# A decoder block on one core: the first stage reads weights, transposes x and starts the projection in another order

## The chip, the core and the metric

The kernel runs on one NeuronCore of a Trainium2 chip. The core has five engines, each with an instruction stream of its own: TensorE (PE, matrix products; the loads of its stationary operand are shown apart as PEld), VectorE (DVE), ScalarE (ACT), GpSimd (POOL) and SyncE (SP), which here only issues DMA transfers. An engine takes its instructions in the order in which they were written for it; they wait for each other through semaphores. The metric is the device time of one execution in microseconds (us).

## The reference

One layer of a hybrid decoder block, for 1024 tokens of width 1024, in float32:

```python
mod = (silu(c) @ w_ada + b_ada)                     # six rows of 1024: sh_a, sc_a, gt_a, sh_m, sc_m, gt_m
h = rms_norm(x, g_attn_pre) * (1 + sc_a) + sh_a
proj = h @ w_in                                     # 1024 -> 2304: qa ka va qb kb vb
... rotary, sliding-window attention A (with sinks), dilated mixture B ...
mixed = concat([rms_norm(oa, g_mix_a), rms_norm(ob, g_mix_b)]); y = mixed @ w_out
x = x + gt_a * rms_norm(y, g_attn_post)
h = rms_norm(x, g_mlp_pre) * (1 + sc_m) + sh_m
y = square(relu(h @ w_up)) @ w_down
x = x + gt_m * rms_norm(y, g_mlp_post)
```

The change touches only what stands first: `sh_a` and `sc_a` (two rows of the product with `w_ada`), the modulated and normalised `h`, and the first sixth of `h @ w_in`.

## The kernel before

The order of all instructions is made by a list scheduler in the kernel's own text (`Sched`): every step is given an engine (or a choice of two), an estimated duration, the steps that it waits for and the buffers that it takes and gives back (`Res`); the scheduler plays the plan through on those estimates and writes the instructions out in the order that results. On the chip each engine then keeps that order whatever the real durations are. TensorE's steps lie in named streams ("xt", "mod", "misc", "dense", "post", "s", "pv" and others), of which the scheduler takes one at a time.

Products in full float32 precision are made of split operands: each operand is written as a high part (`F32R`, a rounded copy) and a low part (the difference), and a product takes three TensorE products, high x high, high x low and low x high (`proj_mm`, lines 769 to 774). For one block of 128 tokens and one chunk k of 128 input channels these are three products of 384 columns, from lines 771, 772 and 774. A projection unit u has 8 blocks and 8 chunks, so 192 of them; there are six units, each with 384 of the 2304 columns.

The first stage (lines 414 to 671) works in these steps:

- `load_x`, `load_ada`, `load_w`: SP brings in the eight blocks of x (512 KB each), the two needed column groups of `w_ada` for each of 8 chunks (1 MB each, two transfers), and the first unit's weights (192 KB each). `load_ada(k)` has four buffers, x has five.
- `x_block(tb)`: ACT squares and sums a block (line 553), DVE and POOL make the reciprocal root (lines 409 and 412), DVE scales the block (558), TensorE transposes it in eight pieces (568, tile `pxt`). For the first five blocks (`FIRST = 5`) ACT copies the pieces to `xnT` (573).
- `mod_chunk(k)`: scale and shift of 128 channels are sums over 1024 rows of `w_ada`. For chunk 0 TensorE does all of them (16 products of one column in the text, line 615, tile `pm`). For chunks 1 to 7 TensorE does two of eight row groups (4 products), DVE multiplies and adds the other six into `acc_a` (lines 626 and 628, 42 instructions of 256 elements), and TensorE sums `acc_a` over partitions with two products against ones (635). DVE finishes scale and shift (640, 641). ACT then modulates five blocks of the chunk (645), ACT writes the high part (651), POOL the low part (654), and the first unit's weights are split by ACT (473) and POOL (478).
- `first_unit`: five accumulators, one bank of PSUM each, take chunk after chunk as its parts come ready (tile `acc`).
- Blocks 5 to 7 of x follow when all chunks are known: they are modulated at the transpose (580, 583) and split whole (593, 596); their 72 projection products are the first tiles of `proj_tile` (tile `pj`).

`evac` empties each finished block (rotary, splitting, transposes to `pq` and `pk` at lines 724 and 736), after which attention for it can begin (scores `s_ps` at line 997, weights `p_sb`, transposes `pt_ps`, outputs `o_ps`). `todo_dense` feeds the remaining projection tiles between the attention work. `next_unit_w` loads and splits the next unit's weights.

Of the kernel before, what the change touches and what calls it, by code (L numbers as in the profile page):

```python
# [10 lines left out]
F32 = mybir.dt.float32  # L11
# [292 lines left out]
def hybrid_block(ctx: ExitStack, tc: tile.TileContext, x, positions, w_ada, b_ada, g_attn_post, w_in, w_out,  # L304
# [110 lines left out]
    FIRST = 5  # L415
# [4 lines left out]
    xnT = p0.tile([P, KC, FIRST * P], F32, name="xnT")  # L420
    r_wa, r_xs, r_acc = Res(4), Res(2), Res(3)
# [6 lines left out]
    e_c = load(lambda: nc.sync.dma_start(head[:], consts[:, 0:HEAD]), 106496, prio=pri())  # L428
    wa_t, wa_e, sent = {}, {}, {}

    def load_ada(k):
        def emit():
            wa_t[k] = p0.tile([P, KC, 2, P], F32, name="wa", tag="wa", bufs=4)
            for i in range(2):
                nc.sync.dma_start(wa_t[k][:, :, i], ada_view[:, :, i * D + k * P:i * D + (k + 1) * P])

        def issued():
            sent[k].t = 0.0
        sent[k] = Ev()
        wa_e[k] = load(emit, 1048576, takes=[(r_wa, 1)], prio=pri(), after=issued)  # L440
# [3 lines left out]
    def load_x(tb, deps=()):  # L444
        r = r_stg if tb % 2 == 0 else r_xs

        def emit():
            x_t[tb] = stage("x_sb") if tb % 2 == 0 else p0.tile([P, D], F32, name="x_sb", tag="x_sb", bufs=2)
            nc.sync.dma_start(x_t[tb][:], x[tb * P:(tb + 1) * P])
        x_e[tb] = load(emit, 524288, deps, takes=[(r, 1)], prio=pri())  # L450
# [3 lines left out]
    def load_w(u, k, prio=None, deps=()):  # L454
# [13 lines left out]
        w_rawe[u, k] = load(emit, 196608, deps, takes=[(r_wst, 1)], prio=pri() if prio is None else prio)  # L468

    def split_w(u, k):  # L470
# [10 lines left out]
        if u == 0:  # L481
            w_e[u, k] = op("POOL", t_ptt(UW), lo(G), [e], gives=[(r_wst, 1)], prio=3)
        else:
            w_e[u, k] = op(("DVE", "POOL"), (t_dv(UW), t_ptt(UW)), (lo(V), lo(G)), [e], gives=[(r_wst, 1)], prio=3)

    for tb in range(2):
        load_x(tb)
    e_posi = load(lambda: nc.sync.dma_start(posi[:], positions), 4096, prio=pri())
    load_ada(0)
    for tb in range(2, FIRST):  # L490
        load_x(tb)
    load_w(0, 0)
    for k in range(1, KC):
        load_ada(k)
        load_w(0, k)
    for tb in range(FIRST, TB):
        load_x(tb, [sent[KC - 2 if tb == FIRST else KC - 1]])

    e_init = op("DVE", 0.3, lambda: (V.memset(ones[:], 1.0), V.memset(nhalf[:], -0.5)), prio=0)
# [40 lines left out]
    def f_sin():  # L540
# [3 lines left out]
    e = op("ACT", 3.0, f_sin, [e], prio=8)  # L544
    e_rope = op("DVE", 0.15, lambda: V.tensor_scalar(sinw[:, :, 0], sinw[:, :, 1], -1.0, None, ALU.mult), [e],
                prio=8)

    e_xn = []

    def x_block(tb):  # L550
# [8 lines left out]
        box, eh, d_all, evs_ = {}, [], [], []  # L559

        def hv():
            return x_t[tb][:].rearrange("p (k t) -> p k t", k=KC)
        r_x_ = r_stg if tb % 2 == 0 else r_xs
        for g in range(2):
            def tr(g=g):
                box[g] = pt.tile([P, 4, P], F32, name="pxt", tag="t")
                for k in range(4):
                    T.transpose(box[g][:, k], x_t[tb][:, (4 * g + k) * P:(4 * g + k + 1) * P], ident)
            d = pe_op("xt", 0.7, tr, [e], takes=[(r_t, 1)], gives=[(r_x_, 1)] if g and tb < FIRST else [])
            d_all.append(d)  # L570
            if tb < FIRST:
                def ev(fn, g=g):
                    return lambda: fn(xnT[:, 4 * g:4 * g + 4, tb * P:(tb + 1) * P], box[g][:])
                e_xn.append(op("ACT", t_ps(512), ev(A.copy), [d], gives=[(r_t, 1)], prio=2))
            else:
                def ev(eng, g=g):
                    def f():
                        for k in range(4 * g, 4 * g + 4):
                            if eng is A:
                                A.activation(hv()[:, k], box[g][:, k - 4 * g], AF.Identity,  # L580
                                             bias=s_a[:, k:k + 1], scale=g_a[:, k:k + 1])
                            else:
                                V.tensor_scalar(hv()[:, k], box[g][:, k - 4 * g], g_a[:, k:k + 1],
                                                s_a[:, k:k + 1], ALU.mult, ALU.add)
                    return f
                evs_.append((d, ev))
        for d, ev in evs_:

            eh.append(op(("ACT", "DVE"), (1.4, 1.3), (ev(A), ev(V)), d_all + [e_gs[k] for k in range(KC)],
                         gives=[(r_t, 1)], prio=1))  # L590
        if tb >= FIRST:
            def hi(fn):
                return lambda: fn(hw[:, tb, 0], x_t[tb][:])

            def lo(eng):
                return lambda: eng.tensor_tensor(hw[:, tb, 1], x_t[tb][:], hw[:, tb, 0].bitcast(F32), ALU.subtract)
            e = op(("ACT", "DVE"), (t_sb(D), t_d2(D)), (hi(A.copy), hi(V.tensor_copy)), eh, prio=1)
            e2 = op(("DVE", "POOL"), (t_dv(D), t_ptt(D)), (lo(V), lo(G)), [e], gives=[(r_x_, 1)], prio=1)
            e_h[tb] = [e, e2]

    e_gs, e_h, e_hh, e_hl = {}, {}, {}, {}
    NF0 = FIRST * P
    ADA_PE = (8, 2, 2, 2, 2, 2, 2, 2)

    def mod_chunk(k):
        b = {}
        e = None
        jp = ADA_PE[k]
        ej = None

        def pm0():
            b["ps"] = px.tile([P, 2], F32, name="pm", tag="x")
            for i in range(2):
                for j in range(jp):
                    T.matmul(b["ps"][:, i:i + 1], wa_t[k][:, j, i], cond[:, j:j + 1], start=(j == 0), stop=(j == jp - 1))  # L615
        if jp:
            e = pe_op("mod", 0.426 * jp, pm0, [wa_e[k], e_cond], takes=[(r_x, 1)],
                      gives=[(r_wa, 1)] if jp == KC else [])
            if jp < KC:
                ej = op("DVE", 0.07, lambda: V.tensor_tensor(bb[:, k], bb[:, k], b["ps"][:], ALU.add), [e, e_cols],  # L620
                        gives=[(r_x, 1)], prio=1)
        for j in range(jp, KC):
            def f(j=j):
                if j == jp:
                    b["acc"] = p0.tile([P, 2, P], F32, name="acc_a", tag="acc_a", bufs=3)
                    V.tensor_scalar(b["acc"][:], wa_t[k][:, j], cond[:, j:j + 1], None, ALU.mult)
                else:
                    V.scalar_tensor_tensor(b["acc"][:], wa_t[k][:, j], cond[:, j:j + 1], b["acc"][:], ALU.mult, ALU.add)  # L628
            e = op("DVE", 0.4 if j > jp else 0.26, f, [wa_e[k], e_cond] if j == jp else [e] + ([ej] if ej and j == KC - 1 else []),
# [1320 lines left out]
```

## Time and profile before

| | us |
|---|---|
| median of three runs | 1196.32 |
| lowest, highest | 1194.2, 1199.15 |
| the profiled execution | 1197.14 |
| its span, first to last instruction | 1195.4 |
| PE busy, PEld busy | 1143.5, 998.0 |
| DVE, ACT, POOL busy | 881.3, 666.6, 264.6 |

In the rows of the profile a group of instructions is named by its line in the kernel, engine, operation, the tile it writes and those it reads, the shape and how often it occurs. In the order of time, the first number is the start in us from the span's start and the second the length of the merged row; what stands in brackets is the idle time of the engine just before and what ended it. In the views by stretches each engine's busy time in the stretch is given with the number of its instructions; PEclk is the share of full speed that TensorE's clock was granted.

### The profile page before, as it was taken

How to read it: one execution, taken by the hardware profiler on the slowest of the kernel's cores; microseconds unless marked ns; L12 is line 12 of the kernel's file. 1: busy time of each engine (PE TensorE's matmuls, PEld its weight loads, DVE VectorE, ACT ScalarE, POOL GpSimd, SP SyncE). 2: the span in 40 equal slices, each digit the busy share in tenths (PEclk: the TensorE clock that was granted, in tenths of full speed). 3: DMA queues.
4: the chain of work that ended last, by engine and by line, in shares of the span. 5: the costliest groups of instructions: out<-in, count | busy, mean ns of one | idle time of the engine just before them, and what ended most of it. 6: DMA issues, size and time to landing. Idle time of an engine off the chain costs nothing.

```text
span 1195.4 us, 17424 instructions
## 1 busy us (share of the span) xinstructions
PE 1143.5 (96%) x6064; PEld 998.0 (83%) x6064; DVE 881.3 (74%) x1794; ACT 666.6 (56%) x1411; POOL 264.6 (22%) x325
## 2 busy tenths in 40 slices
PE   7879999999998998999899999999999999999996
PEld 6869999989998896888688888888888888888885
DVE  4977667666789897667888955479763797646998
ACT  6457666556666787667657533473325643246542
POOL 6534655465655333111100000000000000000002
PEclk9889999999999999999999999999999999999999
DMA  9621333213231422555296126952268511586103
GB/s 290 189 60 60 89 98 97 77 52 102 76 87 54 125 53 77 179 201 204 113 381 246 36 73 238 340 168 62 81 218 284 191 36 53 179 287 220 36 19 141
DMA packets 104423, 166.53 MB, mean 139 GB/s; under 512 B 11152, under 2 KB 56336, under 8 KB 104336
## 3 DMA queue, kind: packets, MB, share of 16 engines
q1 hardware_dynamic: 104336, 165.42, 41.8%
q8 instruction: 48, 0.79, 0.3%
q14 instruction: 39, 0.32, 0.1%
HBM read 137.08 MB, written 28.31 MB: 138 GB/s over the span
## 4 chain that ended last, share of the span: by engine, by line
PE 76%; DVE 13%; issue 4%; ACT 3%; POOL 3%; DMA 1%; SPq 0%; DVEq 0%; POOLq 0%; ACTq 0%
PE mlp_ps L1773 16%; PE mlp_ps L1774 16%; PE mlp_ps L1772 16%; PE pj L771 4%; PE pj L774 3%; PE pj L772 3%; PE s_ps L997 3%; PE o_ps L1131 1%; PE pt_ps L1100 1%; DVE acc_a L628 1%; PE y_ps L1348 1%; PE y_ps L1350 1%; PE pm L615 1%; PE y_ps L1349 1%; PE pt_ps L1103 1%
## 5 line engine op out<-in xcount | busy, mean ns | idle before, releaser
L1772 PE MATMUL mlp_ps<-hw 128*128 128x512 f32 x896 | 350.4, 391 | 0.4 <-ACT hw L1534 0.4
L1773 PE MATMUL mlp_ps<-hw 128*128 128x512 f32 x896 | 349.2, 390 | 1.1 <-DVE hw L1540 1.1
L1774 PE MATMUL mlp_ps<-hw 128*128 128x512 f32 x896 | 349.1, 390 | 0.0
L1773 PEld LDWEIGHTS mlp_ps<-hw 128*128 128x128 f32 x896 | 168.6, 188 | 36.9 <-DVE hw L1540 1.4
L1772 PEld LDWEIGHTS mlp_ps<-hw 128*128 128x128 f32 x896 | 168.6, 188 | 36.1 <-ACT hw L1534 0.8
L1774 PEld LDWEIGHTS mlp_ps<-hw 128*128 128x128 f32 x896 | 168.5, 188 | 35.1
L1543 DVE TENSOR_TENSOR hw<-w,hw 128x1024 fp32r<-128x1024 f32 x96 | 114.6, 1219 | 93.5 <-ACT hw L1536 93.3
L1536 ACT CAST hw<-w 128x1024 fp32r<-128x1024 f32 x96 | 97.4, 1046 | 129.9 <-PE mlp_ps L1774 93.2
L1872 POOL TENSOR_TENSOR st<-st,nhalf 128x1 f32<-128x1 f32 x8 | 7.8, 978 | 602.8 <-DVE st L1870 602.8
L771 PE MATMUL pj<-w_hl,hw 128*128 128x384 f32 x344 | 128.2, 373 | 10.0 <-DVE sk L717 10.0
L774 PE MATMUL pj<-w_hl,hw 128*128 128x384 f32 x344 | 117.4, 341 | 0.0
L772 PE MATMUL pj<-w_hl,hw 128*128 128x384 f32 x344 | 117.1, 341 | 0.0
L1536 ACT CAST hw<-u 128x1024 fp32r<-128x1024 f32 x48 | 48.6, 1051 | 64.6 <-PE mlp_ps L1774 64.6
L1118 DVE TENSOR_TENSOR ph<-pt_ps,ph 128x512 fp32r<-128x512 f32 (+1 forms) x110 | 68.8, 643 | 18.5 <-ACT ph L1114 17.6
L771 PEld LDWEIGHTS pj<-w_hl,hw 128*128 128x128 f32 x344 | 65.8, 191 | 11.8 <-issue 8.7
L1543 DVE TENSOR_TENSOR hw<-u,hw 128x1024 fp32r<-128x1024 f32 x48 | 57.0, 1217 | 18.2 <-ACT hw L1536 18.2
L1114 ACT CAST ph<-pt_ps 128x512 fp32r<-128x512 f32 (+1 forms) x110 | 59.2, 560 | 13.8 <-PE pt_ps L1103 9.8
L772 PEld LDWEIGHTS pj<-w_hl,hw 128*128 128x128 f32 x344 | 66.2, 192 | 0.8 <-issue 0.2
L774 PEld LDWEIGHTS pj<-w_hl,hw 128*128 128x128 f32 x344 | 65.7, 191 | 0.0
L1027 POOL TENSOR_SCALAR p_sb<-p_sb,den 128x128 f32<-128x128 f32 (+3 forms) x64 | 50.1, 786 | 70.2 <-DVE den L1025 46.8
L1830 DVE TENSOR_TENSOR yacc<-yacc,mlp_ps 128x512 f32<-128x512 f32 x96 | 62.1, 680 | 3.3 <-PE mlp_ps L1774 3.3
L1022 ACT ACTIVATE p_sb<-p_sb,mn 128x128 f32<-128x128 f32 (+3 forms) x64 | 49.9, 780 | 20.4 <-DVE mn L1015 16.6
(209 smaller groups left out, 2202.6 us busy)
## 6 DMA issues: line engine op xcount, KB each, us to landing
hw<-s_dram SPq DMA_DIRECT2D x84, 512.0 KB, 4.5
wa_st<-in_w_ada SPq DMA_DIRECT2D x32, 512.0 KB, 4.0
w<-in_w_up SPq DMA_DIRECT2D x32, 512.0 KB, 5.4
w<-in_w_down SPq DMA_DIRECT2D x32, 512.0 KB, 8.0
s_dram<-hw SPq DMA_DIRECT2D x28, 512.0 KB, 4.3
x_sb<-in_x SPq DMA_DIRECT2D x16, 512.0 KB, 6.2
wa<-in_w_ada SPq DMA_DIRECT2D x16, 512.0 KB, 7.0
w_st<-in_w_in SPq DMA_DIRECT2D x32, 192.0 KB, 4.7
```

What stands on the lines that cost most here:

```text
L771: T.matmul(ps, hw[:, tb, 0, t], w[:, 0], start=(k == 0), stop=False)
L772: T.matmul(ps, hw[:, tb, 0, t], w[:, 1], start=False, stop=False)
L774: T.matmul(ps, hw[:, tb, 1, t], w[:, 0], start=False, stop=(k == KC - 1))
L1027: lambda b=b, qi=qi: G.tensor_scalar(rec.p[qi], rec.p[qi], b["den"][:], 1.0, ALU.mult, ALU.mult), [e], prio=1))
L1114: A.copy(b["ph"][:, 0, :w], b["pt"][:, :w])
L1118: V.tensor_tensor(b["ph"][:, 1, :w], b["pt"][:, :w], b["ph"][:, 0, :w].bitcast(F32), ALU.subtract)
L1536: A.copy(out[j][0], flat(src[j]))
L1543: V.tensor_tensor(out[j][1], flat(src[j]), out[j][0].bitcast(F32), ALU.subtract)
L1772: T.matmul(ps[m][:], sh, mh, start=starts and k == 0, stop=False, **kw)
L1773: T.matmul(ps[m][:], sh, ml_, start=False, stop=False, **kw)
L1774: T.matmul(ps[m][:], sl, mh, start=False, stop=k == 3, **kw)
L1830: e = op("DVE", t_dv(512), lambda: V.tensor_tensor(y(), y(), ps[m][:], ALU.add), [e, ml.e_y[tb, n]], gives=gives, prio=1)
```

## The change

- x stays whole in `xnT` (eight blocks instead of five), and all eight blocks go the same way: transposed, copied by ACT or DVE, modulated chunk by chunk. The special path of blocks 5 to 7 is gone. `first_unit` holds eight accumulators side by side (all eight banks of PSUM), and all 192 products of unit 0 are in it.
- Scale and shift are made for pairs of chunks (`mod_group(g)`, four groups). `load_ada(g, j)` brings 512 KB (a quarter of the rows for two chunks of each of scale and shift) in two transfers with runs of 1 KB instead of 512 bytes. For group 0 TensorE does all four quarters (32 products in the text), for groups 1 to 3 two quarters of four (16 products) and the sum over partitions of what DVE did with the other two (4 products). DVE has 12 instructions of 512 elements for this instead of 42 of 256.
- For the first pair, modulation is done in two halves of the blocks. ACT writes the high part straight from `xnT`, DVE (or ACT) then modulates in place, and DVE writes the low part; POOL does neither low parts of h nor those of the first unit's weights.
- Every load of the stage goes through six places of its own and three shared ones, in a fixed turn (`in_turn`), and the second of the loads is now `positions`, ahead of block 1.
- The rotary tables' ACT work comes after the first stage's transposes, and the weights of unit 1 are asked for as soon as the first stage's loads are issued.

```diff
-    FIRST = 5
+    FIRST = 8
+    AHEAD = 6
-    xnT = p0.tile([P, KC, FIRST * P], F32, name="xnT")
-    r_wa, r_xs, r_acc = Res(4), Res(2), Res(3)
+    xnT = p0.tile([P, KC, S], F32, name="xnT")
+    NWA = 6
+    order0 = [("x", t) for t in range(4)] + [(0, j) for j in range(4)] + [("x", t) for t in range(4, TB)]
+    order0 += [(g, j) for g in range(1, 4) for j in range(4)]
+    beside = {a for n, a in enumerate(order0) if n % 3 == 0}
...
+    def load_ada(g, j):
+        def emit():
+            wa_t[g, j] = stage("wa") if (g, j) in beside else place0("wa")
+            for n in range(2):
+                nc.sync.dma_start(
+                    wa_t[g, j][:, 512 * n:512 * n + 512].rearrange("p (i n) -> p i n", i=2),
+                    ada_view[:, 2 * j + n, 0:2 * D].rearrange("p (i n) -> p i n", i=2)[:, :, g * GW:g * GW + GW])
+        wa_e[g, j] = in_turn(emit, 524288, r_in((g, j)))
...
         if u == 0:
-            w_e[u, k] = op("POOL", t_ptt(UW), lo(G), [e], gives=[(r_wst, 1)], prio=3)
+            w_e[u, k] = op("DVE", t_dv(UW), lo(V), [e], gives=[(r_wst, 1)], prio=3)
...
-    ADA_PE = (8, 2, 2, 2, 2, 2, 2, 2)
+    BY_PE = ((0, 1, 2, 3), (2, 3), (2, 3), (2, 3))
+    def mod_group(g):
...
+            def mv(x=x):
+                for k, i in cols4:
+                    for n in range(2 if x >= 0 else 1):
+                        o = GW * i + k * P
+                        w = wa_t[g, x][:, 512 * n + o:512 * n + o + P] if x >= 0 else b["acc"][:, o:o + P]
+                        v = cond[:, 2 * x + n:2 * x + n + 1] if x >= 0 else ones[:, 0:1]
+                        T.matmul(b["ps"][:, 2 * k + i:2 * k + i + 1], w, v, ...)
+            ep = pe_op("mod", 0.9 if x >= 0 else 0.45, mv, ...)
...
+        eh = op("ACT", t_sb(n) + 2 * AP_COST, lambda: A.activation(hh, h, AF.Identity, bias=s_a[:, k:k + 1],
+                                                                  scale=g_a[:, k:k + 1]), deps, prio=0)
+        e = op(("DVE", "ACT"), (t_d2(n) + 2 * AP_DV, t_sb(n) + 2 * AP_COST), (full(V), full(A)), [eh], prio=0)
+        e = op("DVE", t_dv(n), lambda: V.tensor_tensor(hw[:, t0:t1, 1, ks], h, hh.bitcast(F32), ALU.subtract), [e],
+               prio=0)
...
-    acc_at = [(pj, "pj", r_pj)] * 2 + [(po, "o", r_o)] + [(psp, "s", r_s)] * 2
+    acc_at = [(pj, "pj", r_pj)] * 2 + [(po, "o", r_o)] + [(psp, "s", r_s)] * 2 + [(pt, "t", r_t)] * 2 + [(px, "x", r_x)]
...
+        order = [(k, part, tb) for x in (0, 1) for k in range(2) for part in range(2)
+                 for tb in (range(4) if x == 0 else range(4, 7))]
+        order += [(k, part, tb) for k in range(2, AHEAD) for part in range(2) for tb in range(7)]
+        order += [(k, part, 7) for k in range(AHEAD) for part in range(2)]
+        order += [(k, part, tb) for tb in (7, 0, 1, 2, 3, 4, 5, 6) for k in range(AHEAD, KC) for part in range(2)]
```

Counted on TensorE in the built programs: 64 transposes of x in both; products of one column for scale and shift 58 before (44 from line 615, 14 from line 635) and 92 after (80 and 12); projection products of unit 0 ahead of the first tile of `pj` 120 before, 192 after.

262 lines of the change are left out of this document (126 added, 136 removed).

## The prediction

> **What bounds the kernel now.** I read the engines' busy time in five stretches of the span first, then TensorE in order of time where the stretches meet, then the groups by line.
>
> ```profile
> span 1195.4 us, 17424 instructions
> core 0: us, PE busy (x) PEld busy (x) DVE busy (x) ACT busy (x) POOL busy (x), PEclk, DMA share, GB/s
> 7.53:28.70 21.17, 20.09 (x92) 18.82 (x93) 10.34 (x22) 13.22 (x23) 15.79 (x36) 1.00 1.13 310
> 28.70:71.60 42.90, 37.29 (x209) 35.16 (x209) 38.64 (x78) 21.98 (x41) 20.85 (x17) 0.92 0.63 178
> 71.60:77.20 5.60, 0.04 (x2) 0.05 (x1) 5.29 (x28) 2.59 (x15) 3.68 (x2) 0.68 0.00 0
> 77.20:275.50 198.30, 192.75 (x1354) 185.88 (x1355) 138.47 (x484) 126.03 (x381) 101.89 (x113) 0.97 0.27 77
> 275.50:1195.40 919.90, 893.28 (x4413) 758.05 (x4411) 686.27 (x1174) 499.02 (x947) 120.90 (x154) 1.00 0.43 147
> 7.53 2.92 PE L568 MATMUL pxt<-head,x_sb 128*128 128x128 f32 x12 [7.53 <-DVE rs_t L409]
> 10.24 6.83 PE L615 MATMUL pm<-cond,wa 128*128 128x1 f32 x32
> 16.93 4.68 PE L568 MATMUL pxt<-head,x_sb 128*128 128x128 f32 x20
> 21.40 1.71 PE L615 MATMUL pm<-cond,wa 128*128 128x1 f32 x8
> 28.70 0.67 PE L771 MATMUL acc<-w_hl,hw 128*128 128x384 f32 x1
> 29.49 0.52 PE L771 MATMUL acc<-w_hl,hw 128*128 128x384 f32 x1
> 29.81 0.52 PE L772 MATMUL acc<-w_hl,hw 128*128 128x384 f32 x1
> 77.18 0.66 PE L771 MATMUL pj<-w_hl,hw 128*128 128x384 f32 x1 [5.56 <-DVE sk L717]
> 275.02 0.40 PE L1131 MATMUL o_ps<-ph,v_hl 128*128 128x256 f32 x2
> ```
>
> TensorE is busy over nine tenths of every stretch but two: its start, and 71.60 to 77.20, where DVE alone works (5.29 of 5.60). Between 28.70 and 71.60 TensorE and DVE are nearly even. From the o_ps row at 275.02 on, TensorE's order of instructions is the same in both programs to the end, so the 920 us behind it cancel and the difference is settled ahead of that row.
>
> The profiled span is 1195.4 in an execution of 1197.14, 0.82 above the median of 1196.32. I work on the span, and take 0.82 off at the end.
>
> **Paces on TensorE.** Spacing of starts gives the price of a product, at either clock:
>
> ```profile
> 52.10 0.95 PE L615 MATMUL pm<-cond,wa 128*128 128x1 f32 x8
> 52.91 0.42 PE L771 MATMUL acc<-w_hl,hw 128*128 128x384 f32 x1
> 57.71 1.07 PE L568 MATMUL pxt<-head,x_sb 128*128 128x128 f32 x8
> 58.53 0.42 PE L771 MATMUL acc<-w_hl,hw 128*128 128x384 f32 x1
> 62.81 0.33 PE L771 MATMUL acc<-w_hl,hw 128*128 128x384 f32 x1
> 64.37 0.34 PE L772 MATMUL acc<-w_hl,hw 128*128 128x384 f32 x1
> 80.48 0.46 PE L736 MATMUL pk<-ident_r,sk 128*128 128x128 f32 x4
> 80.78 0.41 PE L771 MATMUL pj<-w_hl,hw 128*128 128x384 f32 x1
> L615 PE MATMUL pm<-cond,wa x88: 164/352/370, 10.2 to 57.6; 128*128 128x1 f32 x88
> L635 PE MATMUL pm<-ones,acc_a x28: 165/250/353, 25.5 to 61.4; 128*128 128x1 f32 x28
> ```
>
> A pm pass takes (16.93-10.24)/32 = 0.209 early and (52.91-52.10)/8 = 0.101 late; a transpose of x (21.40-16.93)/20 = 0.224 early, (58.53-57.71)/8 = 0.103 late; a dense product (64.37-62.81)/9 = 0.173 late (nine stand between the two starts) and 29.81-29.49 = 0.32 early; a pk transpose (80.78-80.48)/4 = 0.075. The early ones are half clock. Chunk 0 has 16 pm products in the text and 32 passes in the row, lines 615 and 635 have 44 and 14 against 88 and 28: one product is two passes. So the change takes pm from 58 products (116 passes) to 92 (184). Of L615's passes most ran at half clock: a mean duration of 352 between 164 and 370 says about nine in ten, and L635's 250 under half.
>
> **What the old order would need for the same work.** The new first unit holds all 192 dense products, the old one 120, then 72 more as pj behind the gap. Old order: 77.2 + 72 x 0.173 (12.5) + 12 pq and pk transposes that the new order has inside (0.9) + the restart at half clock, some 11 x (0.32-0.173) = 1.6, gives 92.2. If the new first stage ends at 92.2, nothing is won or lost.
>
> **The new first stage, on TensorE.**
>
> *To the first dense product.* Positions now load ahead of block 1, and three rope steps stand on POOL ahead of the first reciprocal root; behind that root queue DVE's scaling, and behind it the transposes.
>
> ```profile
> 6.12 0.55 POOL L412 TENSOR_TENSOR rstd<-rs_t,nhalf 128x1 f32<-128x1 f32 x1 [5.69 <-DVE rs_t L409]
> 6.63 0.30 POOL L521 TENSOR_TENSOR ang<-posf,head 128x64 f32<-128x64 f32 x1
> 7.66 0.24 POOL L525 TENSOR_SCALAR kq<-kq 128x64 f32<-128x64 f32 x1
> ```
>
> The steps take 7.66+0.24-6.63 = 1.27 if all fall late, 0 if positions come early; I take 0.6: start 8.1. The first dense product now has 32 transposes and all 64 passes of group 0 ahead of it (before, 20 transposes behind 12, and 40 passes of which 32 counted): 32 x 0.224 = 7.2, 64 x 0.209 = 13.4, a wait for the second block 0.4, then scale and shift, one ACT pass over half the blocks, 1.5 together. First dense product 8.1+7.2+13.4+0.4+1.5 = 30.6, against 28.70.
>
> *From there at full pace.* 32 transposes x 0.103 = 3.3; 120 passes x 0.101 = 12.1; 192 dense x 0.173 = 33.2; 12 pq and pk 0.9. Together 49.5.
>
> *Half clock and waits.*
>
> ```profile
> 41.00:43.00 2.00, 2.00 (x8) 0.53 1.04 322
> ```
>
> In the old stage the clock was half again in the midst of dense work (PE 2.00 busy of 2.00 from 41 to 43, but only 8 products, where 2.00/0.173 would be 11, and 0.53 granted). I charge the first 16 dense products with 0.15 each (2.4), 50 of the 120 passes with 0.108 (5.3; the old share behind 28.70 is about 53 of 76), two such dips of 12 products (3.6), and 3 for waits (old: 42.90-37.29 = 5.6 idle; bounds 0 and 5.6). Sum 14.3. The stage ends at 30.6+49.5+14.3 = 94.4.
>
> **DVE, ACT, POOL, SP.** By my sum DVE is not last any more:
>
> ```profile
> L628 DVE SCALAR_TENSOR_TENSOR acc_a<-wa,cond,acc_a x35: 467/485/1785, 21.1 to 60.4; 128x256 f32<-128x256 f32 x35
> L626 DVE TENSOR_SCALAR acc_a<-wa,cond 128x256 f32<-128x256 f32 x7 | 3.2, 461 | 0.0
> L884 DVE SCALAR_TENSOR_TENSOR ada_acc<-wa_st,cond,ada_acc x14: 742/751/753, 662.9 to 816.5; 128x512 f32<-128x512 f32 x14
> L882 DVE TENSOR_SCALAR ada_acc<-wa_st,cond x2: 480/483/486, 662.4 to 752.2; 128x512 f32<-128x512 f32 x2
> L1543 DVE TENSOR_TENSOR hw<-h,hw x10: 1212/1218/1226, 561.9 to 634.4; 128x1024 fp32r<-128x1024 f32 x10
> L558 DVE TENSOR_SCALAR x_sb<-x_sb,rstd x8: 745/764/2043, 6.7 to 64.0; 128x1024 f32<-128x1024 f32 x8
> L478 DVE TENSOR_TENSOR w_hl<-w_st,w_hl x16: 539/596/1482, 107.5 to 388.9; 128x384 fp32r<-128x384 f32 x16
> ```
>
> Removed: at least 35 x 0.485 + 3.2 = 20 us of sums (some stretched to 1.785 beside POOL). Added: three sums at 0.483 and nine at 0.751 = 8.2; low parts of six whole chunks 6 x 1.22 and four halves at about 0.7 = 10.1; in-place modulation, at 0.76 for 1024 columns, 6 x 0.76 + 4 x 0.45 = 6.4; eight weight splits x 0.54 = 4.3; scaling x is in both. That is 9 us more (29 for 20), where the kernel before had 38.64 in 42.90; but the special path of blocks 5 to 7 leaves, and it filled DVE's 5.29 of the 5.60 and part of what precedes. The new DVE work has 30.6 to 94.4 to fit in, twice its length, so I cost it at nothing; without that cover it is rival B. ACT's squares of blocks 4 to 7 now stand behind ACT's first modulation, which waits for group 0; so these blocks' transposes come among the dense products and not ahead, as counted above. SP brings 24 loads of 512 KB and eight of 192 KB, 14.2 MB, in both; at the 310 GB/s of the second stretch that is 46 us, well ahead of 94; what the fixed turn over nine places can cost is rival C.
>
> **Ramp behind it.** 64 score products (s_ps) begin attention.
>
> ```profile
> L997 PE MATMUL s_ps<-kt,qt x64: 220/283/386, 86.8 to 122.0; 128*128 128x256 f32 x50, 128*128 128x128 f32 x14
> 91.00:97.00 6.00, 4.74 (x41) 4.42 (x39) 5.53 (x26) 5.63 (x20) 2.78 (x6) 1.00 0.04 10
> ```
>
> In the old order they stood among 72 dense products, in the new among 51: 21 x 0.173 = 3.6 of cover is gone, while DVE and ACT are nearly full there (5.53 and 5.63 of 6). Bounds 0 and 3.6; I take 1.8.
>
> **Sum.** 94.4 + 1.8 - 92.2 = +4.0: span 1199.4, execution 1201.1, on the median's footing 1196.32 + 4.0 = 1200.3. All passes at full clock behind 28.70, no dips, no waits, no ramp: 4.0 - (14.3 - 2.4) - 1.8 = -9.7, 1186.6. All 120 passes at half (7.6 more), two dips more (3.6), waits 5.6 (2.6 more), full ramp 1.8: +19.6, 1215.9.
>
> **The rivals.**
>
> A, the clock holds: dense work between the pm bursts keeps it up (the burst at 52.10 ran at 0.101 and the product behind it too). Half clock and waits are 3 in place of 14.3: 1200.3-11.3 = 1189.0. Against it the 0.53 at 41 to 43. Chance 0.20.
>
> A2, the clock is full from the start: any passes raise it. The row 7.53 to 21.40 speaks against: 64 instructions without a gap, 11 us from 10.24 on at half pace. Worth 60 x 0.108 + 28 x 0.12 = 9.8 beyond A: about 1179. Chance 0.03. The Trainium skill, "TensorE: Matmul & The Clock Gate" (Part 1, What's actually happening), has the clock go to full after one busy short window of about 3.4 us, whatever the products are; by that rule the 64 passes would run at full clock and this rival would hold. The trace disagrees: 0.209 and 0.224 over all of these rows.
>
> B, slower: DVE becomes last. In-place modulation and low parts of each chunk are one chain on DVE (0.76 + 1.22, where POOL did the lows aside), eight of them, behind sums that were measured stretched up to 1.785. The low product of a chunk then waits. It decides if every chunk is late by over 0.5 us; at 1 us for eight chunks and one dip more (1.8): 1200.3+9.8 = 1210.1. For: DVE was 38.64 of 42.90 and stays loaded; against: the window is longer. Chance 0.27.
>
> C, loads stall: a place is free only when its block is transposed or its quarter summed, and the turn is fixed, so the first quarter of group 3 waits for block 7.
>
> ```profile
> wa<-in_w_ada SPq DMA_DIRECT2D x16, 512.0 KB, 7.0
> ```
>
> One stall is one landing, 7.0 less what lies under TensorE's work: 6, 1206. Chance 0.08.
>
> D, the change isn't as it says: new products are one pass each. 4.0 - 32 x 0.209 - 60 x 0.15 = -11.7 us: 1184.6. Against it the doubled rows. Chance 0.04.
>
> **How the numbers follow.** My forecast has 0.38, spread over 1194 to 1206. A measurement of this kernel tells 0.5% (6 us) from no change: 1190.3 to 1202.3 is "same". Faster: A but for 0.03, with A2 and D, 0.24. Same: that 0.03 and two thirds of the forecast, 0.28. Slower: the rest of the forecast (0.13), B and C, 0.48. The range 1186 to 1213 leaves out A2, D and the far ends of A and B. The forecast's own range is 1194 to 1206.
>
> **What would show it.** Right: 184 passes of pm, at 0.21 in group 0; first acc product at 30 to 31; last acc product at about 94; pj begins without a gap; the o_ps row of 275.02 stands at about 279. Wrong: TensorE waits over 6 us for DVE behind 30 (B); pm passes at 0.101 throughout the dense stretch, end ahead of 86 (A); gaps ahead of pm that end with a load (C); 92 passes (D); or a shift that comes or goes behind 275.

## The result and the profile after

| | before | changed |
|---|---|---|
| median, us (runs) | 1195.53 (4) | 1207.16 (4) |
| lowest to highest | 1194.2 to 1199.15 | 1202.78 to 1208.05 |
| profiled execution, its span | 1197.14, 1195.4 | 1202.78, 1201.0 |
| ratio to before, 95% interval | | 1.0068, 1.004 to 1.0095 |

In a second series, on one chip, the changed kernel had a median of 1204.6 over 10 runs beside 1198.68 over 22 runs of the kernel before, ratio 1.0037 (1.0018 to 1.0057). So by these ratios, which are the record's own with their intervals, it is slower by about half a per cent, 4 to 8 us; the plain quotients of the medians are larger, 1.0097 and 1.0049, 12 and 6 us. Single executions of it differ by up to 10 us. The profiled execution of the first series is its fastest of four.

The stretches of the changed kernel, cut at the places that answer to those shown of before, and TensorE in order of time:

```profile
core 0: us, PE busy (x) PEld busy (x) DVE busy (x) ACT busy (x) POOL busy (x), PEclk, DMA share, GB/s
8.39:30.99 22.60, 20.48 (x96) 19.99 (x97) 5.02 (x14) 7.84 (x14) 9.16 (x28) 1.00 0.78 263
30.99:94.95 63.96, 61.84 (x356) 59.81 (x357) 39.30 (x100) 34.73 (x71) 17.20 (x18) 0.87 0.49 150
94.95:275.33 180.38, 176.23 (x1271) 168.89 (x1270) 130.51 (x460) 119.70 (x365) 88.46 (x101) 1.00 0.25 73
275.33:1201.00 925.67, 897.10 (x4412) 759.94 (x4411) 688.09 (x1176) 499.41 (x951) 121.16 (x154) 0.99 0.42 147
```

```profile
8.39 1.97 PE L592 MATMUL pxt<-head,x_sb 128*128 128x128 f32 x8 [8.39 <-DVE rs_t L409]
12.82 3.41 PE L639 MATMUL pm<-cond,wa 128*128 128x1 f32 x16
16.09 1.95 PE L592 MATMUL pxt<-head,x_sb 128*128 128x128 f32 x8
30.99 0.69 PE L789 MATMUL acc<-w_hl,hw 128*128 128x384 f32 x1 [1.43 <-ACT hw L669]
...
65.23 1.84 PE L639 MATMUL pm<-cond,wa 128*128 128x1 f32 x16
66.94 1.03 PE L639 MATMUL pm<-ones,acc_a 128*128 128x1 f32 x8
67.83 2.22 PE L639 MATMUL pm<-cond,wa 128*128 128x1 f32 x16
...
94.95 0.34 PE L789 MATMUL pj<-w_hl,hw 128*128 128x384 f32 x1
...
275.33 0.40 PE L1162 MATMUL o_ps<-ph,v_hl 128*128 128x256 f32 x2
```

Three things are to be seen. TensorE waits for nearly nothing in the stage (61.84 busy of 63.96), while DVE has 39.30 of work in the same time: TensorE's own work is the bound, and pj begins without a gap at 94.95. Its clock was not full there (0.87). And the row that stood at 275.50 before stands at 275.33: in this pair of profiles the whole loss of 5.6 us lies behind the place from which TensorE's order is the same, 925.67 against 919.90.

The column PEclk is to be read with care at the start. It shows 1.00 wherever no change of the clock has been recorded yet, here up to 35.17 us. Sixteen passes in 12.82 to 16.09 are 0.204 each and the first dense products came 0.32 apart, which are the prices of half clock.

The trace gives the stretches of half clock exactly. All but the one that the end of the execution cuts short are multiples of 3.41 us, and they lie on one grid within an execution. Below, a piece of 3.41 us on this grid is called a window, and a half window is one at half clock:

```profile
45.41:59.06 13.65, 12.26 (x45) 11.55 (x44) 12.60 (x22) 8.31 (x12) 0.00 (x0) 0.50 0.75 229
59.06:69.30 10.24, 10.24 (x83) 10.24 (x81) 3.00 (x7) 3.92 (x4) 0.00 (x0) 1.00 0.06 19
69.30:72.71 3.41, 3.41 (x14) 3.41 (x14) 2.59 (x6) 2.16 (x2) 0.00 (x0) 0.50 0.14 42
```

That is four half windows, three at full clock and one more half window. In the second series' profile of the same kernel there were five and four:

```profile
42.20:59.27 17.07, 15.68 (x65) 15.18 (x65) 11.70 (x21) 9.71 (x15) 0.00 (x0) 0.50 0.70 218
59.27:66.10 6.83, 6.83 (x50) 6.83 (x49) 2.09 (x7) 0.90 (x1) 0.00 (x0) 1.00 0.10 29
66.10:79.75 13.65, 13.65 (x58) 13.65 (x57) 6.16 (x10) 6.74 (x8) 0.00 (x0) 0.50 0.10 30
```

TensorE was busy without a break from 59.27 to 79.75 there; it did 50 instructions in 6.83 us at full and 58 in 13.65 us at half clock. Its pj began at 101.12 in place of 94.95: 6.2 us for four more half windows, 1.5 each. Half of 3.41, or 1.71, is what a half window would cost if TensorE's work were all that counts.

### The profile page after: what moved, and what is told of

Same layout as the page of the kernel before. It is cut to its first block, busy times and chain, and to the rows that moved or that the text cites. A ratio compares the mean times of both kernels' runs of the same rounds, so it can differ in the third digit from the quotient of the medians.

```text
span 1201.0 us, 17539 instructions
## 1 busy us (share of the span) xinstructions
PE 1155.6 (96%) x6132; PEld 1008.6 (84%) x6132; DVE 865.2 (72%) x1760; ACT 665.5 (55%) x1402; POOL 238.3 (20%) x309
## 4 chain that ended last, share of the span: by engine, by line
PE 75%; DVE 11%; issue 3%; ACT 3%; POOL 3%; DMA 2%; SPq 1%; DVEq 0%; POOLq 0%; ACTq 0%
PE mlp_ps L1804 16%; PE mlp_ps L1805 15%; PE mlp_ps L1803 15%; PE pj L789 3%; PE pj L792 3%; PE pj L790 3%; PE s_ps L1028 2%; PE pm L639 2%; PE o_ps L1162 1%; DVE ph L1149 1%; PE pt_ps L1131 1%; PE acc L789 1%; PE acc L790 1%; DMA o_sb<-o_dram 1%; PE acc L792 1%
## 5 line engine op out<-in xcount | busy, mean ns | idle before, releaser
L1574 DVE TENSOR_TENSOR hw<-w,hw 128x1024 fp32r<-128x1024 f32 x96 | 114.8, 1223 | 95.3 <-ACT hw L1567 94.9
L789 PE MATMUL pj<-w_hl,hw 128*128 128x384 f32 x320 | 117.1, 366 | 1.8 <-DVE sk L735 1.8
L792 PE MATMUL pj<-w_hl,hw 128*128 128x384 f32 x320 | 108.0, 337 | 0.0
L790 PE MATMUL pj<-w_hl,hw 128*128 128x384 f32 x320 | 107.6, 336 | 0.0
L789 PEld LDWEIGHTS pj<-w_hl,hw 128*128 128x128 f32 x320 | 60.3, 189 | 2.8 <-DVE sk L735 2.2
L790 PEld LDWEIGHTS pj<-w_hl,hw 128*128 128x128 f32 x320 | 60.5, 189 | 0.7 <-POOL w_hl L506 0.2
L792 PEld LDWEIGHTS pj<-w_hl,hw 128*128 128x128 f32 x320 | 60.0, 188 | 0.0
```

The costliest lines, as they stand in the source:

```text
L789: T.matmul(ps, hw[:, tb, 0, t], w[:, 0], start=(k == 0), stop=False)
L790: T.matmul(ps, hw[:, tb, 0, t], w[:, 1], start=False, stop=False)
L792: T.matmul(ps, hw[:, tb, 1, t], w[:, 0], start=False, stop=(k == KC - 1))
L1574: V.tensor_tensor(out[j][1], flat(src[j]), out[j][0].bitcast(F32), ALU.subtract)
```

## The experiments

All times of a series are from one chip and share the runs of the kernel before, whose median was 1198.68 in the series of "before again", "changed again", "one quarter" and "half of group 0", 1198.17 in that of "both", "spread" and "32 columns", and 1199.22 in that of "one quarter again" and "no quarter". "Windows" are the half windows from the first dense product to the last of unit 0; the last two columns set TensorE's rows against the first profile of before.

| kernel | median, us | ratio to before (interval) | first acc | next unit's first pj | windows | row of 275.50 | from there to the end |
|---|---|---|---|---|---|---|---|
| before again | 1199.49 | 1.0 (0.9987, 1.0013) | 27.35 | | | -1.0 | +3.4 |
| changed, first | 1207.16 | 1.0068 (1.004, 1.0095) | 30.99 | 94.95 | 5 | -0.2 | +5.8 |
| changed again | 1204.6 | 1.0037 (1.0018, 1.0057) | 30.39 | 101.12 | 9 | +6.1 | +4.3 |
| one quarter | 1194.05 | 0.9963 (0.995, 0.9977) | 30.50 | 88.78 | 4 | -5.9 | +5.9 |
| one quarter again | 1194.04 | 0.9955 (0.9939, 0.997) | 30.88 | 89.28 | 4 | -5.4 | +3.0 |
| no quarter | 1198.77 | 0.9995 (0.998, 1.001) | 30.87 | 89.1 | 5 | -0.9 | +5.5 |
| half of group 0 | 1203.65 | 1.0042 (1.0019, 1.0064) | 27.01 | 98.7 | 9 | +3.8 | +7.0 |
| both | 1199.3 | 1.0009 (0.9994, 1.0025) | 27.25 | 88.5 | 5 | -5.2 | +8.1 |
| spread | 1206.53 | 1.0079 (1.0047, 1.0111) | 30.91 | 117.6 | 18 | +20.7 | +3.9 |
| 32 columns | 1202.47 | 1.0037 (1.0014, 1.006) | 30.82 | 94.9 | 4 | -0.3 | +5.7 |

### Both kernels again

No edit.

> The kernel of before once more, for a second profile of it. In the first pair of profiles both kernels stand level at the row from which TensorE's order is the same (275.50 against 275.33), and the 5.6 us of the changed kernel come behind it, with two more windows of 3.41 us at half clock there (455 and 465). Theory W (windows): where a window of half clock falls behind 275 us changes from execution to execution, in this kernel too; this profile then has its half windows behind 275 us at other places than the one at 582, between 0 and 4 of them, and its span is 1181 us plus the clock lost, within 2 us. Theory L (a fixed late cost of the change): this profile has the same single window at 582, and its rows behind 275 us lie within 1 us of the first profile's.

> The changed kernel once more, for a second profile. Theory W: half windows behind 275 us at places other than 455, 465 and 602 or in another number, and span minus lost clock again 1181 to 1184; the kernel's excess over before is then made of windows, mostly in its first 100 us, where it has the longer runs of one-column products (5 half windows between 45 and 73 in the first profile against 4 between 39 and 81 before). Theory L: the same rows at 454 to 470 and at 600 are late again by 4 to 6 us against the kernel of before, wherever the windows are.

Before had windows at 38, 45 and 72 again, at 96 and 243 again, and two new ones at 383 that, with a longer wait just ahead of them, cost 3.4 us. So windows do change between executions. The changed kernel had nine in its stage in place of five, 6.3 us more ahead of the row of 275.50. Behind it the changed kernel lost 4.3 us again, at the first place that theory L names (2.4 us between 440 and 480), but nothing at 600. Span minus lost clock, which I had expected to be constant, isn't a usable measure: where TensorE waits anyway, a slow clock costs little or nothing (0.1 us for the half window at 453 in one of the kernels below).

The second profile of before also shows that the clock can be raised by transposes, ahead of any dense product:

```profile
8.11:10.96 2.85, 2.85 (x14) 2.62 (x14) 0.76 (x2) 1.17 (x2) 2.42 (x8) 1.00 1.07 357
10.96:14.37 3.41, 3.41 (x33) 3.41 (x32) 0.15 (x1) 2.06 (x4) 1.95 (x8) 1.00 1.04 367
14.37:31.44 17.07, 15.20 (x65) 13.75 (x64) 13.27 (x29) 13.57 (x24) 12.30 (x23) 0.50 1.13 290
```

In the first row nothing is recorded yet, and 14 instructions in 2.85 us are at the pace of half clock, 0.20 each. From 10.96 the clock was full; one window of pm passes later (33 instructions in 3.41, 0.10 each) it was half, for five windows. Neither profile of the changed kernel had this early window.

### One quarter of the rows on TensorE

```diff
-    BY_PE = ((0, 1, 2, 3), (2, 3), (2, 3), (2, 3))
+    BY_PE = ((0, 1, 2, 3), (3,), (3,), (3,))
```

> The changed kernel with one quarter of four on TensorE for the groups 1 to 3 in place of two: 48 of 184 passes of pm less on TensorE, six sums of 512 elements more on DVE (6 x 0.75 = 4.5 us). Theory P (TensorE's passes are what the stage lasts): the end of the first unit comes 48 x 0.101 to 48 x 0.209 = 5 to 10 us earlier than 94.95, with 0 to 2 half windows less, and the time is 5 to 10 us below the changed kernel. Theory D (the stage is bound by the chain on DVE and the loads): the end stays within 2 us of 94.95 or comes later, with more idle time of TensorE ahead of acc.

> The kernel with one quarter of four on TensorE for groups 1 to 3 once more, as the measure for the one with the repeats, and a second profile. Theory P: 0.2 to 0.5 per cent below before again (1193 to 1196), end of the first unit at 86 to 92 by the number of windows. If its first time was luck of the windows, it comes at 1198 to 1201.

```profile
88.60 0.35 PE L792 MATMUL acc<-w_hl,hw 128*128 128x384 f32 x1
88.78 0.34 PE L789 MATMUL pj<-w_hl,hw 128*128 128x384 f32 x1
```

The unit ends 6.2 us earlier than in the better profile of the changed kernel, and both series have it about 10 us below the changed kernel's 1204.6 and 0.4% below before (both intervals lie below 1), with its runs closer together (1191.17 to 1197.04 in twelve, against 1197.97 to 1207.65 in ten). Theory P stands, theory D doesn't: DVE had room for 4.5 us of sums. This version beats both kernels.

### No quarter

```diff
-    BY_PE = ((0, 1, 2, 3), (2, 3), (2, 3), (2, 3))
+    BY_PE = ((0, 1, 2, 3), (), (), ())
...
-                                 stop=(x == parts[-1] and n == k == i == 1))
+                                 stop=(x == parts[-1] and k == i == 1 and n == (1 if x >= 0 else 0)))
```

The second edit only marks the last product of a sum, which is now one against `ones`.

> The changed kernel with no quarter on TensorE for groups 1 to 3: only the sums over partitions stay there, 88 passes of pm in place of 136 with one quarter and 184, six more sums of 512 elements on DVE (4.5 us). Theory P: 48 x 0.101 to 0.209 = 5 to 10 us less TensorE work, end of the first unit at 80 to 84, time 5 to 8 us below the kernel with one quarter. Theory D (DVE is last from here on: with one quarter it was busy 18.3 of the 20 us from 50 to 70): TensorE waits ahead of acc for ACT behind DVE, end at 88 or later, time equal to the kernel with one quarter within 2 us or above it.

TensorE's waits and two stretches of this kernel:

```profile
59.59 1.02 PE L639 MATMUL pm<-ones,acc_a 128*128 128x1 f32 x8 [0.70 <-DVE acc_a L622]
62.55 0.69 PE L789 MATMUL acc<-w_hl,hw 128*128 128x384 f32 x1 [1.94 <-ACT hw L669]
```

```profile
50.00:60.00 10.00, 9.30 (x52) 9.01 (x51) 9.89 (x13) 3.52 (x7) 1.20 (x1) 0.93 0.45 128
60.00:70.00 10.00, 8.06 (x31) 7.63 (x31) 9.60 (x19) 4.95 (x5) 1.92 (x1) 0.58 0.14 41
```

DVE is busy 19.49 of 20 us, TensorE waits for its sums and for what follows them, and three half windows stand in the second stretch (0.58). Theory D holds from here on: of none, one and two quarters, one is the best.

### Half of group 0, and both edits

```diff
-    BY_PE = ((0, 1, 2, 3), (2, 3), (2, 3), (2, 3))
+    BY_PE = ((2, 3), (2, 3), (2, 3), (2, 3))
```

> The changed kernel with two quarters of four on TensorE for group 0 too: 64 passes of pm become 40 there, four sums more on DVE, which has 3.6 us of work in the 20 us ahead of 30. Theory P: 24 passes at half clock, 24 x 0.209 = 5 us, leave the way to the first dense product, which comes at 26 in place of 30.99, and the end and the time 4 to 6 us earlier. Theory D: DVE's sums, or the loads, end last in the start too, and the first dense product stays at 30 or later, the time within 2 us of the changed kernel.

The second kernel has `((2, 3), (3,), (3,), (3,))`.

> The changed kernel with one quarter on TensorE for groups 1 to 3 and two for group 0: the two edits of the two kernels before it (one quarter, 1194.05; half of group 0, 1203.65) together, 112 passes of pm in place of 184. Theory P (passes of TensorE at whatever clock is granted): first dense product at 27, end of the first unit at about 88.6 - 3.5 = 85, time 1190 to 1193. Theory W (the number of windows at half clock decides, and the start of group 0 only moves where they fall): first dense product at 27, but the end within 2 us of 88.6 and the time 1193 to 1196. Theory D (DVE is last by now): end at 90 or later with idle TensorE ahead of acc.

With half of group 0 the first dense product came at 27.01, about where theory P had it (26):

```profile
27.01 0.69 PE L789 MATMUL acc<-w_hl,hw 128*128 128x384 f32 x1 [1.39 <-ACT hw L669]
```

The end did not follow. With nine windows the unit ended at 98.7, and the time was within 1 us of the changed kernel's in its series. In the kernel with both edits it ended at 88.5, where the one with one quarter ended with the later start. So the 3 to 4 us won at the start were gone at the end twice, in one case with more half windows (nine, against five in the changed kernel's first profile), in the other with one half window more than with the single edit, which pays for half of it. The rest is open. At 1199.3 the kernel with both edits is 5 us slower than the one with the single edit. In the profiles that lies behind the row of 275.50 (+8.1 against +5.9 and +3.0), where the one of both edits has six half windows; why it has them is open too.

### Spreading the one-column products

```diff
-            ep = pe_op("mod", 0.9 if x >= 0 else 0.45, mv, ...)
+            for q, ki in enumerate(cols4 if g else [None]):
...
+                ep = pe_op("mod", (0.9 if x >= 0 else 0.45) / (4 if g else 1), ...,
+                           ... + ([gap[0]] if g else []), ..., after=done)
```

For groups 1 to 3 each piece of two products waits, in the scheduler's plan, until 0.3 us behind the piece before, so that dense products come between.

> The changed kernel with the pm products of groups 1 to 3 spread in pairs among the dense products, nothing else changed: 184 passes as before. Theory W (a window that is filled mostly by one-column passes is followed by one at half clock): fewer windows at half clock between 40 and 95, 1 to 3 in place of 5 and 9 in the two profiles, the end of the first unit at 88 to 92 in place of 94.8 and 100.9, time 3 to 8 us below the changed kernel. Theory P: same passes, same time within 2 us. Theory D: the later end of a group's sums delays ACT's modulation, idle time ahead of acc grows, and the time is 2 us or more above.

The profile went the other way from what theory W forecast:

```profile
42.38:103.82 61.44, 60.88 (x232) 60.82 (x232) 20.62 (x36) 19.13 (x27) 2.83 (x3) 0.50 0.27 80
```

```profile
79.05 0.85 PE L641 MATMUL pm<-cond,wa 128*128 128x1 f32 x4
79.75 1.31 PE L802 MATMUL acc<-w_hl,hw 128*128 128x384 f32 x3
80.86 0.85 PE L641 MATMUL pm<-cond,wa 128*128 128x1 f32 x4
```

Eighteen half windows in a row, TensorE busy 60.88 of 61.44 us and nowhere near an idle window: here 0.7 us of one-column passes stand beside 1.1 us of dense products, and the clock doesn't come back until the last pm is through. A burst can cost the clock once, but the windows of dense products alone behind it were followed by full clock. Theory W's form of "a window mostly filled with one-column passes" falls.

What fits is the number of columns that stream through TensorE. A dense product of 384 columns takes 0.32 us at half clock, so a half window holds 3.41/0.32 x 384, some 4,100. Sixty half windows of the fourteen traces hold dense products and pm passes only, with TensorE busy over 97% of the time. The 31 with at most 2,983 columns were followed by another half window, the 29 with at least 3,017 by full clock. At full clock no such line shows: some windows with many passes were followed by half clock and others not.

The profiled execution, 1221.71, is far from the median of its runs, 1206.53, which suggests fewer half windows in most of them; only this one was traced. By the medians spreading is no gain, and its loss against the changed kernel isn't clear: the ratios to before, 1.0079 and 1.0037, have overlapping intervals.

### A wider moving operand

```diff
+    cond32 = const.tile([P, KC, 32], F32, name="cond32")
...
-                        v = cond[:, 2 * x + n:2 * x + n + 1] if x >= 0 else ones[:, 0:1]
-                        T.matmul(b["ps"][:, 2 * k + i:2 * k + i + 1], w, v, ...)
+                        v = cond32[:, 2 * x + n] if x >= 0 else ones[:, 0:32]
+                        T.matmul(b["ps"][:, 32 * (2 * k + i):32 * (2 * k + i) + 32], w, v, ...)
```

> The changed kernel with 32 equal columns as the moving operand of each pm product in place of one: same number of passes, TensorE streams more. Theory W in the form that the columns streamed are what keeps the clock: the early passes of group 0 come at 0.10 to 0.13 in place of 0.209, fewer windows at half clock in all, end of the first unit 3 to 8 us earlier. In the form that 32 columns are still too few: pace 0.20 to 0.23 early, windows as before (5 to 9), time 0 to 4 us above the changed kernel for the longer passes.

```profile
12.61 3.46 PE L642 MATMUL pm<-cond,wa 128*128 128x32 f32 x16
15.88 1.95 PE L595 MATMUL pxt<-head,x_sb 128*128 128x128 f32 x8
```

(15.88-12.61)/16 = 0.204 a pass: 32 columns cost no more than one and didn't raise the clock early. The stage ended at 94.9 with four windows, as with one column and five. The second form of the theory holds: 32 columns are too few to matter.

### The late loss: a shift against the grid

The thin end of attention lies at 440 to 480. To see whether the loss there depends on how the grid of windows falls on it, a dense product was repeated at the head of a projection tile, which only takes time:

```diff
                 if k == 0:
                     b.append(pj.tile([P, 512], F32, name="pj", tag="pj"))
+                    if (u, tb) == (4, 4):
+                        for _ in range(14):
+                            T.matmul(b[0][:, :UW], hw[:, tb, 0, 0:P], w_hl[u, 0][:, 0], start=True, stop=True)
```

Five times at unit 3 and, in another kernel, at unit 4 in the kernel of before; 14 times in the kernel with one quarter.

> The kernel of before with five repeats of a dense product at the head of one tile of the unit 3 projection, 5 x 0.173 = 0.87 us of TensorE, nothing else: a shift in time of all that follows. Theory G (the late loss is where the grid of 3.41 us windows falls on the thin stretch at 440 to 480: both profiles of before have the first y_ps product 1.5 us into a window and no half window there, the profiles of the changed kernel and its two variants have it at 0.9, 2.0, 2.5 and 2.8 and have one to three): the shift puts it near 2.4, half windows appear between 448 and 470, and the time is 2 to 5 us above before. Theory L (the late loss is a property of the change): time 0.9 above before, within 1, and no half window at 448 to 470 unless the grid stands elsewhere for another reason.

> The kernel of before with the five repeats of a dense product at unit 4, fourth tile (350 us), behind all windows that the earlier place of the repeats had met (there, at 244, the shift took one half window away), nothing else. Theory G (the late loss is where the grid of windows falls on the thin stretch): three profiles of before and of its shifted form have the first y_ps product 1.3 to 1.6 us into a window, with none or one half window at 448 to 470; this shift puts it at 2.2 to 2.5, where the changed kernel and its variants have two or three; so two or three half windows between 448 and 475, 2 to 4 us lost there, time 3 to 5 us above before (1201 to 1203). Theory L (the late loss comes of the change itself): the time is 0.9 us above before, none or one half window there.

> The kernel with one quarter on TensorE for groups 1 to 3, with 14 repeats of a dense product at the same place (350 us): 14 x 0.173 = 2.4 us of useless work, nothing else. Its profile had the first y_ps product at 2.5 us into a window, and three half windows at 448 to 465 that cost 4.3 us against before. Theory G: 2.5 + 2.4 = 4.9, less 3.41 = 1.5 us into a window, as in before; the late loss goes, and the added work is paid back: between 2 us below and 1 us above the same kernel without the repeats. Theory L: 2.4 us above it, with the half windows still there.

| kernel | median, us | beside | half windows, 440 to 480 |
|---|---|---|---|
| before, 5 at unit 3 | 1198.88 | before 1198.17 | 1 |
| before, 5 at unit 4 | 1201.67 | before 1199.22 | 2 |
| one quarter, 14 at unit 4 | 1198.24 | without them 1194.04 | 2 |

Theory G found no support. The useless work was not paid back: 4.2 us for 2.4 of it. Both shifts in before met half windows there, one (453 to 457) that cost 0.1 and two that cost 1.0; the 2.5 us of the second shift (ratio 1.0018, 0.9999 to 1.0038) are not clear of the 0.9 of plain work. But the grid didn't fall as I had reckoned, since a window met or missed on the way moves all that follows: the first y_ps product stood 1.3, 1.2 and 2.3 us into a window, where 2.4, 2.2 to 2.5 and 1.5 were meant. So theory G was not tested as it was meant to be, and what speaks against it is a wait that all profiles of the changed kernel and its variants share.

The loss itself can be measured product by product, since TensorE's 4,411 products from the row of 275.50 on are the same in all these kernels (added ones left out). Between 440 and 480 the ten profiles of the changed kernel and its variants lose 1.9 to 4.2 us against the first profile of before, the other three of before and its shifted forms 0.1 to 1.1.

What theory L had right can be read in the traces. In the kernel before, all engines in order of time (SPq is SP's queue of transfers: start, and how long SP was held by it):

```profile
453.14 0.55 SPq L1247 DMA_DIRECT2D gate_a<-gate_d  x1
...
453.50 2.38 POOL L1232 TENSOR_TENSOR hw<-wo_st,hw 128x1024 fp32r<-128x1024 f32 x1
...
453.86 0.38 SPq L1293 DMA_DIRECT2D o_sb<-o_dram  x1
...
459.48 1.05 ACT L1306 CAST oh<-o_sb 128x1024 fp32r<-128x1024 f32 x1
...
460.85 0.40 PE L1348 MATMUL y_ps<-hw,oh 128*128 128x512 f32 x1
```

and the same rows of the changed one:

```profile
454.95 2.37 POOL L1263 TENSOR_TENSOR hw<-wo_st,hw 128x1024 fp32r<-128x1024 f32 x1
...
457.34 0.33 SPq L1278 DMA_DIRECT2D gate_a<-gate_d  x1
...
457.84 0.38 SPq L1324 DMA_DIRECT2D o_sb<-o_dram  x1
...
462.76 1.04 ACT L1337 CAST oh<-o_sb 128x1024 fp32r<-128x1024 f32 x1 [1.72 <-DMA o_sb<-o_dram]
...
463.85 0.50 PE L1379 MATMUL y_ps<-hw,oh 128*128 128x512 f32 x1 [1.40 <-ACT oh L1337]
```

Before, SP sends gate_a ahead of POOL's last product with `wo_st`. After, it sends it 0.02 us behind the end of that product (454.95 + 2.37 = 457.32). SP stands still, the load of `o_sb` behind it in the queue is late, ACT idles 1.72 for it and TensorE 1.40. All ten profiles of the changed kernel and its variants show this (ACT idle 0.8 to 2.0 ahead of `oh`, gate_a 0.02 to 0.03 behind POOL), none of the four of before and its shifted forms does. TensorE itself idled for it in eight of the ten, 0.5 to 1.7 us. A half window follows the wait in six of them (465 in the first profile). The order can't be the reason: behind 283 us all five engines, SP's queue among them, have the same order in both kernels.

A second, smaller wait of this kind stands near 293. It is shown for before and then for the changed kernel:

```profile
293.08 0.95 PE L903 MATMUL ada_ps<-ones,ada_acc 128*128 128x1 f32 x8
293.57 1.05 PE L934 MATMUL ada_ps<-ones,ada_acc 128*128 128x1 f32 x8 [0.32 <-POOL ada_acc L918]
```

TensorE waits 0.3 to 1.3 us there in all ten profiles and 0 to 0.3 in the four. What delays POOL was not followed up.

Why SP waits ahead of `gate_a` can be worked out from the code. `gate_a` is the first tile of a ring laid over the freed staging places, of which there are three, used in turn. The first stage took four of them before (blocks 0, 2, 4, 6) and takes eight after (`beside`: every third of 24 loads). Four and eight leave 1 and 2 over three, so every later tenant of the staging sits one place on, and by this count `gate_a` now lies where the last `wo_st` was. This is argued from the code; a kernel that uses seven or ten places in the first stage, which would put it back, was not tried.

## Why the prediction was right or wrong

*Sign and size.* +4.0 us and 1200.3 were forecast; the ratio of 1.0068 is +8.1 on 1196.32 (4.8 to 11.4), that of the second series +4.4. The direction and the range of 1186 to 1213 hold, and the forecast is at the low end: of its own range, 1194 to 1206, the first series' median of 1207.16 lies just outside and the second's 1204.6 inside. That the total came near is in part luck, since in the first pair the whole difference lay behind the place where the forecast had put none.

*Start.* POOL's first reciprocal root came at 7.00 (6.12 before), the transposes at 8.39 where 8.1 was forecast, the first dense product at 30.99 where 30.6 was. Right.

```profile
7.00 0.55 POOL L412 TENSOR_TENSOR rstd<-rs_t,nhalf 128x1 f32<-128x1 f32 x1
```

*Passes.* Two records for each product, no fewer:

```profile
L639 PE MATMUL pm<-cond,wa x160: 165/250/353, 12.8 to 69.7; 128*128 128x1 f32 x160
```

with 24 of the sums, 184 in all; rival D is out. Between 12.82 and 16.09 sixteen passes took 0.204 each.

*The end of the stage.* 94.4 was the sum, 94.95 the first profile. The 14.3 for half clock and waits was 94.95 - 30.99 - 49.5 = 14.5, of which 2.1 was waiting (63.96 - 61.84), five half windows could cost 5 x 1.71 = 8.5, and the products up to 35.17, at half clock, (35.17 - 30.99)/2 = 2.1. Some 1.8 stays open. It was nevertheless one draw: the second profile needs 101.12 - 30.39 - 49.5 = 21.2, with nine half windows. The term was right in one execution and a third too small in the other. Of the 120 pm passes behind the first dense product 50 had been charged at half clock; 18 ran so in the first profile and 76 in the second. The 50 rested on a misread row: in `x88: 164/352/370` the middle number is the median and not the mean, and 50 of these 88 passes, not nine in ten, took over 0.3 us. Of the 64 behind 28.70 in before four came at 0.21, where "53 of 76" was assumed. So that the term fitted once was luck.

*DVE, rival B.* DVE did 39.30 of work in 63.96 us and TensorE waited 2.1 in all; the low parts waited for nothing worth a line. Rival B's time was near, its mechanism wrong. A form of it, DVE last by its sums, became true only with no quarter on TensorE. (One reading beside it was off: TensorE was busy 37.29 of 42.90 us between 28.70 and 71.60, which is under nine tenths; nothing in the sum hangs on it.)

*Loads, rival C.* TensorE's waits in the stage, 1.4 us the longest, end with ACT, not with a load.

*The clock, rivals A and A2.* A needed 3 us where 14.5 were lost. For A2, TensorE's passes of group 0 came at 0.204 throughout. The Trainium skill, "TensorE: Matmul & The Clock Gate" (Part 1, What's actually happening), gives a free-running window of 3413 ns and throttling after an idle window. By the first half of that rule the trace agrees: every stretch at half clock but the last is a multiple of 3.41 us, on a grid that stands differently in each execution. By the second it doesn't: eighteen windows at half clock with TensorE busy 60.88 of 61.44 us.

*Ramp, and what cancels.* Against 92.2 the stage lost 2.8 us, yet the row of 275.50 came at 275.33, where +4.0 was forecast. Before had two half windows on that way (97 and 244) and the changed profile none, which at 1.5 each would be about 3 us. In the second profile the row was 6.1 late. So the sum at this place was neither confirmed nor refuted by one profile; it is between -0.2 and +6.1, with +4.0 inside.

*The step that failed* is the first one: "the 920 us behind it cancel". TensorE's order is the same from the row of 275.50 on (not quite from 275.02, where three pj products stand at another place), but 3.0 to 8.1 us were lost behind it in ten of ten profiles of the changed kernel and its variants, and 0 to 3.4 in before, its repeat and its shifted forms (added products taken off). Part of this is half windows, which come and go from execution to execution; what sets the ten apart is the 1.9 to 4.2 us between 440 and 480. I compared the order of the instructions and not what each transfer waits for. What SP waits for ahead of `gate_a` had changed, which the order doesn't show; that a place in the staging is the reason is argued and not shown. By the first series the forecast was too small by 4.1 us, about this loss; by the second it was too small by 0.4 only.

## What to carry to other kernels

Two programs with the same order of instructions can still differ in their waits: where a change alters how often a shared ring of buffers is used, look at who lies in which place later, down to the far end of the kernel. Work of one column on TensorE costs its own time and can cost the clock of its neighbours, so put as much of it on an engine with room as that engine can take. Spreading what remains held the clock down in the one execution that was traced; in bursts it left windows of dense products alone behind it. Where a kernel's stages hang on the clock, one profile of each version isn't a measure of a stage: here two profiles of one kernel differed by 6 us at the same row.

## What the hardware showed that was not expected

A TensorE that is busy all the time can stay at half clock for 61 us while all windows but the last hold some one-column passes (the kernel with the spread products). Sixty half windows of dense products and such passes parted at about 3,000 columns of some 4,100: below, the clock stayed at half, above, it rose. The clock fell to half behind a window of such passes in which TensorE had no gap (65.23 to 69.91 in the changed kernel, half from 69.30). Products with 32 columns moved at the same 0.204 as those with one. And a window at half clock cost between 0.1 us, in the thin end of attention, and about 1.7 where TensorE was the bound: (116.24 - 94.77)/13 = 1.65 by the last acc rows, over the thirteen half windows that the spread kernel had more than the changed one.
